# Ten expert chunks issued inside the key search, keys prepared a tile ahead, and shorter runs in the one-hot layout

## The chip, the cores and the metric

The kernel runs on one core of a Trainium2 chip. Its engines are TensorE (PE, matrix products), VectorE (DVE), ScalarE (ACT), GpSimd (POOL) and SyncE (SP, which issues most of the transfers). The metric is the device time of one execution in microseconds, as the median of several runs.

## The reference, cut to what matters

One layer of a transformer-like block: two attention branches and their projections, then a product-key expert layer (PEER). The change lies in the second half. Each of 512 tokens of width 1024 looks up 16 of 16384 experts for each of 8 heads:

```python
def peer_ffn(x, w_q, sub_keys, u, v):          # x: rms-normed tokens
    q = (xb @ w_q).reshape(PEER_BLOCK, PEER_HEADS, 2, PEER_HALF)
    scores = jnp.einsum('thpd,hpkd->thpk', q, sub_keys)
    top_s, top_i = lax.top_k(scores, PEER_TOPK)
    cand_s = top_s[:, :, 0, :, None] + top_s[:, :, 1, None, :]
    cand_i = top_i[:, :, 0, :, None] * PEER_N_KEYS + top_i[:, :, 1, None, :]
    best_s, best_pos = lax.top_k(cand_s, PEER_TOPK)
    expert = jnp.take_along_axis(cand_i, best_pos, axis=-1)
    gate = jax.nn.softmax(best_s, axis=-1)
    act = jax.nn.gelu(jnp.einsum('thkd,td->thk', u[expert], xb), approximate=False)
    return jnp.einsum('thk,thkd->td', (gate * act), v[expert])
```

An expert's number is 128 times its first key plus its second. All is in float32.

## The kernel before

The 512 tokens are four tiles of 128. One tile (`GT`) fetches its experts' rows by indirect transfers, which POOL issues and DVE multiplies. The other three (`DT`, `T` = 384 tokens together) are done densely: all 16384 experts are multiplied for all 384 tokens, 128 experts at a time, and a gate matrix that is zero for experts not chosen selects. A float32 product is three matmuls (`mm3`, L145 to L150) of operands split into a high and a low part: ACT copies the high part, and DVE or POOL subtracts it (`split`, L673 and L674).

**First product, a chunk (`first`).** For one of 128 values `i2` of the one key, a tile `ut` of 512 KB comes over SP's queue (two buffers). ACT makes `uh` in two halves, POOL or DVE makes `ul`, PE forms `pa` in 24 matmuls of 384 columns, and ACT applies the Gelu and writes `ga`. `more(n)` runs the next n chunks ahead of the last loop, with `ul` on POOL. The results `ga` of `AHEAD` = 37 such chunks are kept in SBUF.

**The search** (L582 to L598). For each of 16 chunks `c` of `w_q`: 24 matmuls `mm` of 512 columns, a copy on ACT, four score products `tp<-kt,s` (L592), a copy on ACT, then DVE finds the best sixteen for each tile of tokens (`top16`, L564 to L568), and after every second `c` the best sixteen sums of two keys (`best_sums`).

**Index arithmetic** (L611 to L636). The gate's softmax, with an exponential on ACT (L612), and the positions of the best sums as small integers.

**Retrieval** (`retrieve`, one tile of tokens at a time). ACT spreads positions (`oh`, L646), DVE compares (L647) and multiplies by the keys' numbers (L649), and a tree of four additions (L652, L653) sums 16 places into `ia` and `ib`. After every third step of this generator a chunk is issued: 2 + 8 = 10 chunks in all.

**Token blocks** (L715 to L754). For each dense tile PE transposes keys and gate, ACT makes `sel` of them (L720), and DVE cuts the gate into power of two and two mantissa parts (L725 to L730). Then for each of 8 blocks of 16 tokens DVE makes five tensors of 2048 elements: `o2` (L738), two `ow` (L740), `o1` (L741) and `o1` times `power` (L742). Their layout is (16/`TI`, 128, `TI`), so runs of `TI` = 4 tokens lie side by side. PE multiplies them in 32 matmuls `pg` (L747), which put each gate in its place in the 128 × 128 matrix of experts, ACT copies the matrix out (L750, L751), and SP writes `stage` to DRAM (`spool`). One chunk is issued after every block: 24. Three more follow.

**Last loop** (L799 to L820). For each of the 128 values: `vt` comes in, the gates are multiplied with `ga`, and 18 matmuls `acc` of 512 columns sum the output, with one further chunk beside it while there are some left (91 of 128).

The order of instructions on each engine is set by a scheduler that starts from the order in which the program issues them; each engine works through its own list in order.

Of the kernel before, what the change touches and what calls it, by code (L numbers as in the profile page):

```python
# [8 lines left out]
F32 = mybir.dt.float32  # L9
F32R = mybir.dt.float32r  # L10
# [21 lines left out]
TB = 16  # L32
TI = 4
AHEAD = 37
S2, GAT, WB, UB, VB = 8, 4, 3, 3, 3
# [12 lines left out]
def block_kernel(ctx, tc, x, mix_gain, w_in, gate_bias, q_gain, k_gain, sinks, w_up_a, w_up_b, w_out,  # L48
# [12 lines left out]
    wk = scope(mix, "wk", 2)  # L61
    grp = scope(mix, "grp")
    pmm = scope(mix, "pmm", 4, space=PSUM)
    ptp = scope(mix, "ptp", 2, space=PSUM)
    pz = scope(mix, "pz", 2, space=PSUM)
    gated = ctx.enter_context(ExitStack())
# [503 lines left out]
    def best_sums(h):  # L570
# [8 lines left out]
        for r in range(NT):  # L579
            top16(cs[:, r, :], top[:, r, h, :], pos[:, r, h, :])  # L580

    kt = None  # L582
    norm2(0)
    for c, ps in colsT(w_q, 0, 16, h2T, KD, G, lambda: norm2(1)):
# [15 lines left out]
    dram = ctx.enter_context(tc.tile_pool(name="dram", bufs=1, space=bass.MemoryType.DRAM))  # L600
    xkeep = dram.tile([len(DT), P, D], F32, name="xkeep")
    for i, j in enumerate(DT):
        nc.sync.dma_start(xkeep[i], X[:, NT - 1 - j, :])
    XG = {j: gwk.tile([P, D], F32, name=f"xg{j}") for j in GT}
    for j in GT:
        nc.sync.dma_start(XG[j], X[:, NT - 1 - j, :])
    mix.close()
# [30 lines left out]
    def retrieve(j):  # L638
# [21 lines left out]

    T = P * len(DT)
    SP = P - RES
    upool = scope(ctx, "upool", 2)
    pa_ = scope(ctx, "pa", 2, space=PSUM)
# [3 lines left out]
    def split(pool, src, name, eng, bufs):  # L668

        res = []  # L670
        for b in range(2):
            hi, lo = (pool.tile([P, KD // 2, P], F32R, name=name + n, tag=name + n, bufs=bufs) for n in ("h", "l"))
            A.activation(hi, src[:, 4 * b:4 * b + 4], AF.Copy)  # L673
            eng.tensor_tensor(out=lo, in0=src[:, 4 * b:4 * b + 4], in1=hi.bitcast(F32), op=OP.subtract)  # L674
            res.append((hi, lo))
        return res

    def first(i2, eng=G):

        ut = us.tile([P, KD, P], F32, name="ut", tag="ut", bufs=2)  # L680
        nc.sync.dma_start(ut, peer_ut[i2])
        u = split(us, ut, "u", eng, UB)
        pa = pa_.tile([P, 512], F32, name="pa", tag="pa")
        for k in range(KD):
            mm3(pa[:, :T], u[k // 4], h2T, (SL, k % 4, SL), (SL, k, slice(0, T)), k == 0, k == KD - 1)
        ga = upool.tile([P, T], F32, name="ga", tag="ga", bufs=AHEAD)
        A.activation(ga, pa[:, :T], AF.Gelu)
        return ga

    ahead = {}  # L690

    def more(n):
        for i2 in range(len(ahead), min(len(ahead) + n, AHEAD)):
            ahead[i2] = first(i2)
# [9 lines left out]
    with ExitStack() as st:  # L704
# [9 lines left out]

        for j in DT:  # L715
            pt = pg.tile([P, 4, P], F32, name="pg", tag="pg")
            for i in range(3):
                nc.tensor.transpose(pt[:, i, :], KEYS[j][i].rearrange("p h k -> p (h k)"), ident)
            sel = bw.tile([P, 2, P], F16, name="sel", tag="sel")
            A.activation(sel, pt[:, 0:2, :], AF.Copy)  # L720

            part = bw.tile([P, 2, P], F16, name="part", tag="part")
            two, man = (bw.tile([P, P], F32, name=n, tag=n) for n in ("two", "man"))
            power = bw.tile([P, P], BF16, name="power", tag="power")
            V.tensor_scalar(two.bitcast(I32), pt[:, 2, :].bitcast(I32), 0x7F800000, None, op0=OP.bitwise_and)  # L725
# [3 lines left out]
            V.tensor_copy(part[:, 0, :], man)  # L729
            V.tensor_tensor(out=part[:, 1, :], in0=man, in1=part[:, 0, :], op=OP.subtract)  # L730
            for tb in range(P // TB):
                tg = (NT - 1 - j) * (P // TB) + tb
# [132 lines left out]
```

## Time and profile before

| what | value |
|---|---|
| runs | 1726.94, 1725.89, 1722.54 us; median 1725.89 |
| profiled execution | 1720.6 us; its span 1718.9 us |
| PE busy | 1651.5 us, 96% of the span |
| DVE, ACT, POOL busy | 1282.0 (75%), 745.8 (43%), 582.7 (34%) |
| chain that ended last | PE 81%, DVE 13%, issue 3% |

The chain is followed back from the last instruction, at each step to what released it. "Busy" is the time in which an engine carries out instructions that the profile counts. The clock in a row of windows is the one granted to PE, as a share of 2.4 GHz. In a row of waits the engine and line that waited stand first, behind the arrow the one that ended the wait, then the total in us, the number of waits and the longest.

### The profile page before, as it was taken

Reading aid. Unit: us, or ns where it says so; the run is one execution under the profiler, and the core shown is the slowest. Engines: PE = TensorE matmul, PEld = TensorE weight load, DVE = VectorE, ACT = ScalarE, POOL = GpSimd, SP = SyncE. Lnnn points to the kernel's source line nnn. Section 1 sums busy time; section 2 is a strip of 40 time slices with the busy share of each in tenths; the row PEclk is TensorE's granted clock in tenths of the full one; section 3 lists DMA queues with packets and bytes.
Section 4 is the critical chain, followed back from the end, with each engine's and each line's share of the span. In section 5 each row is a group of like instructions: output and inputs, shape, how many; then the busy total and the mean of one; then the engine's idle time right before and its main releaser. Section 6 shows DMA issues by size and latency. Waiting matters only on the chain.

```text
span 1718.9 us, 24631 instructions
## 1 busy us (share of the span) xinstructions
PE 1651.5 (96%) x8969; PEld 1466.4 (85%) x8969; DVE 1282.0 (75%) x2471; ACT 745.8 (43%) x1457; POOL 582.7 (34%) x446
## 2 busy tenths in 40 slices
PE   6999999999996899989999999999999999999998
PEld 5887777798885798989999999999999999998886
DVE  5444345635999998898897878777777777877874
ACT  4557635533324454545344343343344434443442
POOL 4100011512323654453343434334444343433310
PEclk9999999999998899999999999999999999999999
DMA  4321231123301364657999988888988888877874
GB/s 159 98 75 50 73 89 59 62 87 125 108 1 62 107 205 145 208 171 244 406 372 344 323 277 314 319 290 318 322 281 313 316 295 310 290 269 248 294 234 145
DMA packets 158347, 361.29 MB, mean 210 GB/s; under 512 B 10385, under 2 KB 86161, under 8 KB 156305
## 3 DMA queue, kind: packets, MB, share of 16 engines
q1 hardware_dynamic: 120496, 224.94, 37.5%
q0 software_dynamic: 36864, 134.23, 23.5%
q8 instruction: 70, 1.15, 0.3%
q10 hardware_dynamic: 864, 0.54, 0.1%
q14 instruction: 53, 0.43, 0.1%
HBM read 331.89 MB, written 27.26 MB: 209 GB/s over the span
## 4 chain that ended last, share of the span: by engine, by line
PE 81%; DVE 13%; issue 3%; ACT 1%; POOL 1%; DMA 0%; DVEq 0%; SPq 0%; ACTq 0%; POOLq 0%
PE acc L148 10%; PE acc L150 10%; PE acc L149 10%; PE pa L148 9%; PE pa L150 9%; PE pa L149 9%; PE pg L747 5%; PE mm L149 5%; PE mm L150 5%; PE mm L148 5%; DVE tt L566 1%; PE z L462 1%; DVE oh L652 1%; PE mm L490 1%; DVE idx L568 1%
## 5 line engine op out<-in xcount | busy, mean ns | idle before, releaser
L148 PE MATMUL pa<-h2Th,uh 128*128 128x384 f32 x1024 | 349.3, 341 | 17.6 <-ACT uh L673 17.2
L150 PE MATMUL pa<-h2Th,ul 128*128 128x384 f32 x1024 | 349.6, 341 | 6.8 <-POOL ul L674 6.8
L149 PE MATMUL pa<-h2Tl,uh 128*128 128x384 f32 x1024 | 348.3, 340 | 0.0
L673 ACT ACTIVATE uh<-ut 128x512 fp32r<-128x512 f32 x256 | 160.9, 632 | 323.4 <-PE pa L149 237.1
L148 PE MATMUL acc<-vh,wh 128*128 128x512 f32 x768 | 301.1, 392 | 0.0
L150 PE MATMUL acc<-vh,wl 128*128 128x512 f32 x768 | 299.9, 390 | 0.0
L149 PE MATMUL acc<-vl,wh 128*128 128x512 f32 x768 | 298.6, 389 | 0.0
L762 POOL DMA_INDIRECT row<-peer_u,ex x128 | 175.2, 1369 | 250.0 <-DVE row L774 193.8
L762 POOL DMA_INDIRECT row<-peer_v,ex x128 | 166.5, 1301 | 267.4 <-DVE xg L784 193.0
L673 ACT ACTIVATE vh<-vt 128x512 fp32r<-128x512 f32 x256 | 159.8, 624 | 140.3 <-PE acc L150 136.5
L148 PEld LDWEIGHTS pa<-h2Th,uh 128*128 128x128 f32 x1024 | 195.6, 191 | 23.5 <-ACT uh L673 19.0
L150 PEld LDWEIGHTS pa<-h2Th,ul 128*128 128x128 f32 x1024 | 195.3, 191 | 8.8 <-POOL ul L674 8.8
L149 PEld LDWEIGHTS pa<-h2Tl,uh 128*128 128x128 f32 x1024 | 195.3, 191 | 3.7
L674 POOL TENSOR_TENSOR ul<-ut,uh 128x512 fp32r<-128x512 f32 x74 | 137.0, 1860 | 172.4 <-ACT uh L673 165.4
L674 DVE TENSOR_TENSOR vl<-vt,vh 128x512 fp32r<-128x512 f32 x256 | 176.6, 690 | 23.5 <-ACT vh L673 22.0
L674 DVE TENSOR_TENSOR ul<-ut,uh 128x512 fp32r<-128x512 f32 x182 | 125.5, 690 | 85.4 <-ACT uh L673 85.4
L150 PEld LDWEIGHTS acc<-vh,wl 128*128 128x128 f32 x768 | 144.1, 188 | 32.5
L149 PEld LDWEIGHTS acc<-vl,wh 128*128 128x128 f32 x768 | 144.2, 188 | 27.3
L148 PEld LDWEIGHTS acc<-vh,wh 128*128 128x128 f32 x768 | 144.2, 188 | 26.3
L784 DVE SCALAR_TENSOR_TENSOR xg<-row,wt,xg 128x1024 f32<-128x1024 f32 x128 | 163.7, 1279 | 1.3
L774 DVE SCALAR_TENSOR_TENSOR row<-row,h 128x1024 f32<-128x1024 f32 x128 | 151.4, 1219 | 4.8 <-DMA row<-peer_u,ex 4.7
L158 DVE TENSOR_TENSOR wlo<-w,whi 128x1024 fp32r<-128x1024 f32 x52 | 64.9, 1250 | 85.9 <-ACT whi L157 81.7
(232 smaller groups left out, 2823.5 us busy)
## 6 DMA issues: line engine op xcount, KB each, us to landing
ut<-peer_ut SPq DMA_DIRECT2D x128, 512.0 KB, 4.9
vt<-peer_v SPq DMA_DIRECT2D x128, 512.0 KB, 6.9
spool<-stage SPq DMA_DIRECT2D x24, 960.0 KB, 5.0
gs<-spool SPq DMA_DIRECT2D x15, 1536.0 KB, 9.7
w<-w_in SPq DMA_DIRECT2D x17, 1024.0 KB, 5.4
w<-w_q SPq DMA_DIRECT2D x8, 1024.0 KB, 5.6
w<-w_out SPq DMA_DIRECT2D x4, 1024.0 KB, 5.1
x<-x SPq DMA_DIRECT2D x4, 512.0 KB, 5.8
```

The source lines that it names most:

```text
L148: nc.tensor.matmul(ps, lhsT=l[0][li], rhs=r[0][ri], start=start, stop=False)
L149: nc.tensor.matmul(ps, lhsT=l[0][li], rhs=r[1][ri], start=False, stop=False)
L150: nc.tensor.matmul(ps, lhsT=l[1][li], rhs=r[0][ri], start=False, stop=stop)
L158: eng.tensor_tensor(out=lo, in0=raw, in1=hi.bitcast(F32), op=OP.subtract))
L462: nc.tensor.matmul(z[:, :nk], lhsT=qT[:, h, cols(NT - 1 - j)], rhs=kbT[:, h // 2, row0(j):S], start=True, stop=True)
L490: nc.tensor.matmul(PY[j][s * 64:(s + 1) * 64, h // 2, :], lhsT=vb[:, NT - 1 - j + b, h * DH:(h + 1) * DH], rhs=lt[:, b, :], start=(b == 0) ...
L673: A.activation(hi, src[:, 4 * b:4 * b + 4], AF.Copy)
L674: eng.tensor_tensor(out=lo, in0=src[:, 4 * b:4 * b + 4], in1=hi.bitcast(F32), op=OP.subtract)
L747: nc.tensor.matmul(pp[:, i, :], lhsT=o1[:, q, :, i], rhs=ow[:, s, q, :, i], start=(s == 0), stop=(s == 1))
L762: G.indirect_dma_start(out=t, out_offset=None, in_=src, in_offset=bass.IndirectOffsetOnAxis(ap=ex[:, h, k:k + 1], axis=0))
L774: V.scalar_tensor_tensor(out=t, in0=t, scalar=1.0, in1=h2, op0=OP.mult, op1=OP.mult, accum_out=wt[:, h, k:k + 1]))
L784: V.scalar_tensor_tensor(out=xj, in0=t, scalar=wt[:, h, k:k + 1], in1=xj, op0=OP.mult, op1=OP.add))
```

## The change

`EARLY` = 10 chunks are issued in the search, one after each of `c` = 4 to 13. Their `ga` lie in a pool of their own, `early`, where the rows of the residual (`X`, pool `grp`) lay. For that, the rows are copied out (`xkeep`, `xg`) ahead of the second norm, and their pool has a stack of its own that ends there. The PSUM pool of `pa` opens before the search, in the place of a pool of the attention that now closes earlier. The tree of four additions becomes one `tensor_reduce`. In the retrieval a chunk is issued after every second step, 2 + 12 = 14 in all. In the token blocks it is one after every second block, 12 in all, with `ul` on DVE; two more follow, so `AHEAD` is 38. The preparation of keys is now a function, `parts`, which is called for the next tile in the fourth block of the one before, with two buffers for what it makes. The layout's `TI` falls from 4 to 2; the matmuls of `pg` still come four tokens at a time.

```diff
-TI = 4
-AHEAD = 37
+TI = 2
+AHEAD = 38
+EARLY = 10
...
     gated.close()
+    early = scope(ctx, "early", side="right")
     us = scope(ctx, "us", 2, side="right")
+    pa_ = scope(ctx, "pa", 2, space=PSUM, side="right")
...
+        if i2 % AHEAD < EARLY:
+            ga = early.tile([P, T], F32, name="ga", tag="ga", bufs=EARLY)
+        else:
+            ga = upool.tile([P, T], F32, name="ga", tag="ga", bufs=AHEAD - EARLY)
...
         if c % 2:
             best_sums(c // 2)
+        if 4 <= c < 4 + EARLY:
+            more(1)
     mix.close()
...
-            for n in (8, 4, 2):
-                V.tensor_tensor(out=oh[:, :, :, 0:n], in0=oh[:, :, :, 0:n], in1=oh[:, :, :, n:2 * n], op=OP.add)
-            V.tensor_tensor(out=dst, in0=oh[:, :, :, 0], in1=oh[:, :, :, 1], op=OP.add)
+            V.tensor_reduce(out=dst, in_=oh, axis=AX.X, op=OP.add)
...
     more(2)
     for j in DT + GT:
         for i, _ in enumerate(retrieve(j)):
-            if i % 3 == 0:
+            if i % 2 == 0:
                 more(1)
...
-        for j in DT:
+        def parts(j):
+
...
+            return sel, part, power
+
+        now = parts(DT[0])
+        for n, j in enumerate(DT):
+            sel, part, power = now
             for tb in range(P // TB):
...
-                more(1)
+                if tb % 2 == 0:
+                    more(1, V)
+                if tb == 3 and n + 1 < len(DT):
+                    now = parts(DT[n + 1])
```

Three places in the order. On PE in the search, around the score product (`tp<-kt,s`) of a late `c`; before:

```order
L150 MATMUL mm<-h2Th,wlo 128x512
L148 MATMUL mm<-h2Th,whi 128x512
L592 MATMUL tp<-kt,s_4807 128x128 x4
L149 MATMUL mm<-h2Tl,whi 128x512
L150 MATMUL mm<-h2Th,wlo 128x512
```
After, the same place for `c` = 13:

```order
L152 MATMUL mm<-h2Tl,whi 128x512
L153 MATMUL mm<-h2Th,wlo 128x512
L151 MATMUL pa<-h2Th,uh 128x384
L152 MATMUL pa<-h2Tl,uh 128x384
L153 MATMUL pa<-h2Th,ul 128x384
L151 MATMUL pa<-h2Th,uh 128x384
L643 MATMUL tp<-kt,s_5156 128x128 x4
```
The score products stood among `mm` matmuls alone; now they stand among `pa` matmuls of a chunk, 244 of which come before the last score product.

On DVE in the retrieval, the first tile; before (`i16` holds the places 0 to 15, `idf` the keys' numbers):

```order
L647 TENSOR_TENSOR oh_5146<-oh_5146,i16_3676 128x2048
L649 TENSOR_TENSOR oh_5146<-oh_5146,idf_5043 128x2048
L652 TENSOR_TENSOR oh_5146<-oh_5146 128x128x8
L652 TENSOR_TENSOR oh_5146<-oh_5146 128x128x4
L647 TENSOR_TENSOR oh_5191<-oh_5191,i16_3676 128x2048
L652 TENSOR_TENSOR oh_5146<-oh_5146 128x128x2
L649 TENSOR_TENSOR oh_5191<-oh_5191,idf_5043 128x2048
L653 TENSOR_TENSOR ia1_5144<-oh_5146 128x128
```
After:

```order
L692 TENSOR_TENSOR oh_5519<-oh_5519,i16_3692 128x2048
L694 TENSOR_TENSOR oh_5519<-oh_5519,idf_5419 128x2048
L692 TENSOR_TENSOR oh_5598<-oh_5598,i16_3692 128x2048
L696 TENSOR_REDUCE ia1_5517<-oh_5519 128x128
L694 TENSOR_TENSOR oh_5598<-oh_5598,idf_5419 128x2048
L696 TENSOR_REDUCE ib1_5518<-oh_5598 128x128
```
The four additions of a tree are replaced by one row, and less stands between the products of one half and of the next.

On DVE in the token blocks; before, two blocks:

```order
L740 TENSOR_TENSOR ow_5723<-o2_5722,part_5529 128x2048 x2
L741 TENSOR_TENSOR o1_5721<-rep_5521,sel_5527 128x2048
L738 TENSOR_TENSOR o2_5813<-rep_5521,sel_5527 128x2048
L742 TENSOR_TENSOR o1_5721<-o1_5721,power_5532 128x2048
L740 TENSOR_TENSOR ow_5814<-o2_5813,part_5529 128x2048 x2
L741 TENSOR_TENSOR o1_5812<-rep_5521,sel_5527 128x2048
```
After, from the third block's products on:

```order
L759 TENSOR_TENSOR ow_6183<-o2_6182,part_6026 128x2048 x2
L760 TENSOR_TENSOR o1_6181<-rep_6018,sel_6024 128x2048
L608 TENSOR_TENSOR ul_6240<-ut_6233,uh_6239 128x512
L761 TENSOR_TENSOR o1_6181<-o1_6181,power_6029 128x2048
L757 TENSOR_TENSOR o2_6273<-rep_6018,sel_6024 128x2048
L760 TENSOR_TENSOR o1_6272<-rep_6018,sel_6024 128x2048
L759 TENSOR_TENSOR ow_6274<-o2_6273,part_6026 128x2048 x2
L761 TENSOR_TENSOR o1_6272<-o1_6272,power_6029 128x2048
```
And on ACT after, ahead of these blocks, with the first copy of `gres` that belongs to them:

```order
L734 ACTIVATE sel_6024<-pg_6020 128x256
L607 ACTIVATE uh_6239<-ut_6233 128x512
L607 ACTIVATE uh_6395<-ut_6393 128x512
L624 ACTIVATE ga_6123<-pa_6098 128x384
L607 ACTIVATE uh_6399<-ut_6393 128x512
L770 ACTIVATE gres_5441<-pg_6044 128x8x4
L771 ACTIVATE stage_6035<-pg_6044 128x120x4
```
The row of `ul` stands among the products of DVE, where none stood; the `uh` that it reads (6239) stands on ACT ahead of the copies of the first block.

## Rows read from the trace of the kernel before

**Rows 1.** Busy us (x instructions) of PE, PEld, DVE, ACT, POOL; clock; DMA, by stage.

```profile
417.00:525.00 108.00, 107.11 (x548) 90.28 (x547) 105.64 (x733) 35.65 (x51) 34.66 (x17) 1.00 0.20 64
525.00:593.00 68.00, 44.05 (x199) 40.06 (x198) 65.21 (x124) 30.33 (x38) 33.89 (x19) 0.80 0.21 69
593.00:798.00 205.00, 191.75 (x1337) 186.04 (x1336) 185.99 (x137) 101.34 (x264) 99.18 (x52) 0.95 0.62 183
```

**Rows 2.** Waits in 510 to 798: us in total, times, longest.

```profile
PE pa L148 <- ACT uh L673: 17.2, 5, 10.2
...
ACT gate L612 <- DVE gate L611: 13.0, 1, 13.0
PE pg L747 <- DVE o L742: 12.8, 3, 5.3
DVE two L725 <- ACT sel L720: 12.6, 2, 6.8
```

**Rows 3.** A 5-us window after the search, columns as in rows 1.

```profile
530.00:535.00 5.00, 0.00 (x0) 0.00 (x0) 4.93 (x36) 0.58 (x2) 0.00 (x0) 0.50 0.00 0
```

**Rows 4.** PE timeline at three edges: start, us, what.

```profile
509.70 1.16 PE L592 MATMUL tp<-kt,s 128*128 128x128 f32 x8 [0.75 <-ACT s L589]
...
793.77 3.93 PE L747 MATMUL pg<-ow,o 128*128 128x128 f16 x32
...
810.89 0.40 PE L148 MATMUL acc<-vh,wh 128*128 128x512 f32 x1
```

**Rows 5.** DVE timeline at the edges of the stages.

```profile
523.93 0.47 DVE L564 MAX8 vals<-s 128x8 f32<-128x128 f32 x2
...
533.72 0.67 DVE L611 TENSOR_TENSOR gate<-top 128x512 f32<-128x512 f32 x1
...
540.42 1.21 DVE L647 TENSOR_TENSOR oh<-oh,i 128x2048 bf16<-128x2048 bf16 x1
...
593.49 0.28 DVE L725 TENSOR_SCALAR two<-pg 128x128 int32<-128x128 int32 x1
```

**Rows 6.** DVE and POOL timelines in the first token blocks.

```profile
607.82 1.21 DVE L741 TENSOR_TENSOR o<-rep,sel 128x2048 bf16<-128x2048 f16 x1
608.95 1.21 DVE L738 TENSOR_TENSOR o<-rep,sel 128x2048 f16<-128x2048 f16 x1
...
602.24 2.28 DVE L742 TENSOR_TENSOR o<-o,power 128x2048 bf16<-128x2048 bf16 x1
...
602.03 1.41 POOL L674 TENSOR_TENSOR ul<-ut,uh 128x512 fp32r<-128x512 f32 x1
```

**Rows 7.** Groups of DVE in 593 to 798: busy us, mean ns, idle before.

```profile
L740 DVE TENSOR_TENSOR ow<-o,part 128x2048 f16<-128x2048 f16 x48 | 85.9, 1827 | 1.0 <-PE pg L747 1.0
```

**Rows 8.** Last loop, tile wh, with and without chunks: min/median/max ns, first and last start.

```profile
L814 ACT ACTIVATE wh<-ga x3: 525/525/527, 1005.6 to 1022.2; 128x384 fp32r<-128x384 f32 x3
...
L814 ACT ACTIVATE wh<-ga x3: 525/525/527, 1560.8 to 1569.0; 128x384 fp32r<-128x384 f32 x3
```

**Rows 9.** Groups of DVE in 533 to 593.5.

```profile
L652 DVE TENSOR_TENSOR oh<-oh 128x1024 bf16<-128x1024 bf16 x8 | 9.8, 1219 | 0.0
...
L652 DVE TENSOR_TENSOR oh<-oh 128x512 bf16<-128x512 bf16 x8 | 6.8, 854 | 0.1
L652 DVE TENSOR_TENSOR oh<-oh 128x256 bf16<-128x256 bf16 x8 | 6.8, 845 | 0.0
L653 DVE TENSOR_TENSOR ia<-oh 128x128 f32<-128x128 bf16 x4 | 2.8, 693 | 0.0
L653 DVE TENSOR_TENSOR ib<-oh 128x128 f32<-128x128 bf16 x4 | 1.8, 438 | 0.1
...
L614 DVE TENSOR_REDUCE gsum<-gate 128x32 f32<-128x512 f32 x1 | 0.7, 677 | 0.0
```

**Rows 10.** Section 5 of the page: the splits of ut on POOL and DVE.

```profile
L674 POOL TENSOR_TENSOR ul<-ut,uh 128x512 fp32r<-128x512 f32 x74 | 137.0, 1860 | 172.4 <-ACT uh L673 165.4
...
L674 DVE TENSOR_TENSOR ul<-ut,uh 128x512 fp32r<-128x512 f32 x182 | 125.5, 690 | 85.4 <-ACT uh L673 85.4
```

More of the change, by code (lines that the diff above doesn't have):

```diff
@@ L61, in block_kernel @@
     wk = scope(mix, "wk", 2)
-    grp = scope(mix, "grp")
+    xrows = ctx.enter_context(ExitStack())
+    grp = scope(xrows, "grp")
     pmm = scope(mix, "pmm", 4, space=PSUM)
     ptp = scope(mix, "ptp", 2, space=PSUM)
-    pz = scope(mix, "pz", 2, space=PSUM)
+    zs = ctx.enter_context(ExitStack())
+    pz = scope(zs, "pz", 2, space=PSUM)
     gated = ctx.enter_context(ExitStack())
@@ L501, in block_kernel @@
     attn.close()
+    zs.close()
     gwk = scope(ctx, "gwk", side="right")
@@ L542, in block_kernel @@
     run(rows(w_out, 0, D, mg, o_done))
+    dram = ctx.enter_context(tc.tile_pool(name="dram", bufs=1, space=bass.MemoryType.DRAM))
+    xkeep = dram.tile([len(DT), P, D], F32, name="xkeep")
+    for i, j in enumerate(DT):
+        nc.sync.dma_start(xkeep[i], X[:, NT - 1 - j, :])
+    XG = {j: gwk.tile([P, D], F32, name=f"xg{j}") for j in GT}
+    for j in GT:
+        nc.sync.dma_start(XG[j], X[:, NT - 1 - j, :])
+    xrows.close()
     def norm2(p):
@@ L580, in best_sums, with split, first, more @@
             top16(cs[:, r, :], top[:, r, h, :], pos[:, r, h, :])
+    T = P * len(DT)
+    upool = None
+    def split(pool, src, name, eng, bufs):
+        res = []
+        for b in range(2):
+            hi, lo = (pool.tile([P, KD // 2, P], F32R, name=name + n, tag=name + n, bufs=bufs) for n in ("h", "l"))
+            A.activation(hi, src[:, 4 * b:4 * b + 4], AF.Copy)
+            eng.tensor_tensor(out=lo, in0=src[:, 4 * b:4 * b + 4], in1=hi.bitcast(F32), op=OP.subtract)
+            res.append((hi, lo))
+        return res
+    def first(i2, eng=G):
+        ut = us.tile([P, KD, P], F32, name="ut", tag="ut", bufs=2)
+        nc.sync.dma_start(ut, peer_ut[i2])
+        u = split(us, ut, "u", eng, UB)
+        pa = pa_.tile([P, 512], F32, name="pa", tag="pa")
+        for k in range(KD):
+            mm3(pa[:, :T], u[k // 4], h2T, (SL, k % 4, SL), (SL, k, slice(0, T)), k == 0, k == KD - 1)
+        if i2 % AHEAD < EARLY:
+            ga = early.tile([P, T], F32, name="ga", tag="ga", bufs=EARLY)
+        else:
+            ga = upool.tile([P, T], F32, name="ga", tag="ga", bufs=AHEAD - EARLY)
+        A.activation(ga, pa[:, :T], AF.Gelu)
+        return ga
+    ahead = {}
+    def more(n, eng=G):
+        for i2 in range(len(ahead), min(len(ahead) + n, AHEAD)):
+            ahead[i2] = first(i2, eng)
     kt = None
@@ L598, in block_kernel @@
             best_sums(c // 2)
[L600 to L606, printed above, removed]
+        if 4 <= c < 4 + EARLY:
+            more(1)
     mix.close()
@@ L658, in retrieve @@
             V.scalar_tensor_tensor(out=ROWS[j], in0=ib, scalar=128.0, in1=ia, op0=OP.mult, op1=OP.add)
-    T = P * len(DT)
     SP = P - RES
     upool = scope(ctx, "upool", 2)
-    pa_ = scope(ctx, "pa", 2, space=PSUM)
     gres = upool.tile([P, RES, T], F32, name="gres", bufs=1)
     spool = dram.tile([SP // OCT, P, T // TB, OCT, TB], F32, name="spool")
[L668 to L694, printed above, removed]
     more(2)
@@ L718, in block_kernel @@
                 nc.tensor.transpose(pt[:, i, :], KEYS[j][i].rearrange("p h k -> p (h k)"), ident)
-            sel = bw.tile([P, 2, P], F16, name="sel", tag="sel")
+            sel = bw.tile([P, 2, P], F16, name="sel", tag="sel", bufs=2)
             A.activation(sel, pt[:, 0:2, :], AF.Copy)
-            part = bw.tile([P, 2, P], F16, name="part", tag="part")
+            part = bw.tile([P, 2, P], F16, name="part", tag="part", bufs=2)
             two, man = (bw.tile([P, P], F32, name=n, tag=n) for n in ("two", "man"))
-            power = bw.tile([P, P], BF16, name="power", tag="power")
+            power = bw.tile([P, P], BF16, name="power", tag="power", bufs=2)
             V.tensor_scalar(two.bitcast(I32), pt[:, 2, :].bitcast(I32), 0x7F800000, None, op0=OP.bitwise_and)
@@ L742, in block_kernel @@
                 V.tensor_tensor(out=o1, in0=o1, in1=spread(power[:, ts]), op=OP.mult)
-                for q in range(TB // TI):
-                    pp = pg.tile([P, TI, P], F32, name="pg", tag="pg")
-                    for i in range(TI):
+                for q in range(TB // 4):
+                    pp = pg.tile([P, 4, P], F32, name="pg", tag="pg")
+                    for i in range(4):
+                        t, k = divmod(4 * q + i, TI)
                         for s in range(2):
-                            nc.tensor.matmul(pp[:, i, :], lhsT=o1[:, q, :, i], rhs=ow[:, s, q, :, i],
+                            nc.tensor.matmul(pp[:, i, :], lhsT=o1[:, t, :, k], rhs=ow[:, s, t, :, k],
                                              start=(s == 0), stop=(s == 1))
```

## Prediction

> **What bounds the kernel now.** I read the stage windows first, then the waits between 510 and 798 us, then the timelines of TensorE (PE) and VectorE (DVE) at the stages' edges. The kernel is a PE kernel with one hole. In [rows 1] three stretches stand under one another. While the best keys are sought (417 to 525) PE is busy for 107.11 of 108 us, and so is DVE, with 105.64. In 525 to 593 (index arithmetic and retrieval) PE is busy for only 44.05 of 68 us, at a mean clock of 0.80. In 593 to 798 (token blocks) it is 191.75 of 205 at 0.95. So of these 381 us PE lies idle for 38, and further time goes at the lower clock. The waits say whose fault that is: PE waits 17.2 us for ACT's `uh` in 5 pieces, the longest 10.2, and 12.8 us for DVE's `o` in 3 pieces [rows 2]. The long one is a chain: ACT has the gate's exponential in its queue and waits 13.0 us for DVE's gate [rows 2], the `uh` stand behind it, and PE does nothing in 530 to 535, where the clock is 0.50, which is 1.2 GHz [rows 3].
>
> DVE is why. The last score product on PE ends at 510.9 (509.70 + 1.16) [rows 4], but DVE only begins the last chunk's top sixteen at 523.93 and the gate at 533.72 [rows 5]: it is behind by 22.9 us, 9.8 of it for that last chunk and its best sums. After that DVE does index arithmetic to 540.42 and the retrieval to 593.49 [rows 5], and the token blocks run until PE's last `pg` row, at 793.77 for 3.93 us, ends at 797.7. The first `acc` follows at 810.89 [rows 4], 13.2 us later, and from there on PE is full.
>
> DVE in the token blocks is slowed by POOL. A 2048-element operation takes 1.21 us (starts 1.13 apart, 607.82 and 608.95) where POOL is idle, and 2.28 at 602.24, where POOL splits `ul` from 602.03 on [rows 6]. The mean of the `ow` products is 1.827 us [rows 7].
>
> **The change part by part.** All is reckoned against the profiled run's own 1720.6 us (span 1718.9); the median of the runs, 1725.89, is 5.3 above it.
>
> *A chunk's price on PE.* In the last loop the `wh` of one expert block follows the last by 8.3 us while a chunk is among them (1005.6 to 1022.2, two steps) and by 4.1 after the last chunk (1560.8 to 1569.0) [rows 8]. A chunk of 24 `pa` matmuls is thus 4.2 us, 0.174 each.
>
> *Ten chunks into the search.* The order shows 244 `pa` matmuls ahead of the last score product, none before. They add 244 × 0.174 = 42.5 us to a stage in which PE was full, so that product ends at 553.4 instead of 510.9. DVE's work there stays the same, some 106 us, but now has 150 to be done in, so its lag falls to the last chunk's own: 0.7 for ACT's copy and 9.8, that is 10.5 instead of 22.9, a gain of 12.4. The POOL splits (two an iteration, of 1.4 us each [rows 6]) and ACT's two `uh` lie beside PE's 10.7 us an iteration. The ten `ut` transfers stand behind `w_q`'s on SP; they are asked for long ahead, so I cost them at nothing. If that cover fails, it is rival D. The moved `xkeep` and `xg` transfers read finished rows and cost nothing.
>
> *Index arithmetic* stays at 6.7 us (533.72 to 540.42).
>
> *Retrieval, 53.1 us before.* Eight trees of four adds took 9.8 + 6.8 + 6.8 + 2.8 + 1.8 = 28.0 us, 3.5 each [rows 9], beside POOL. One `tensor_reduce` over 2048 elements does not occur before. The nearest row reduces 512 in 0.677 us [rows 9], so four times that, 2.7, is the upper end; the 1.21 of a 2048-element product is the lower end, 1.2. I take 2.5, near the upper one since it is the same operation: −1.0 × 8 = −8. Were the adds free of POOL (3.5 × 1.21 / 2.28 = 1.9), the reduce would cost 0.6 × 8 = 5 us more than they do; POOL keeps its splits in this stage, so I don't take that. Now three chunks go with each tile. PE needs 14 × 4.2 = 59 us for the stage's 14 chunks, POOL 28 splits at 1.86 [rows 10] = 52, and from 553.4 to the loop's start DVE needs 10.5 + 6.7 + 45 = 62. They are so close that ACT's queue will couple them: I give back 3 (my estimate) and take 48 for the retrieval, a gain of 5.
>
> The Trainium skill ("VectorE: DVE Perf Modes", Rules for kernel authors) calls `tensor_reduce` the slowest operation of DVE, to be expected at one element a cycle, and advises restructuring, which speaks against this edit. By that rule the reduce would be some 2.2 us, an estimate, and the sum would fall by 2 more, since the adds it replaces are held up by POOL here.
>
> *Token blocks, 593.5 to 797.7 = 204.2 us before.* The splits of the twelve chunks left here move from POOL to DVE. 24 blocks × 5 operations × 1.135 = 136.3. Of the 24 `ul` 21 stand inside the loop at 0.69 [rows 10] = 14.5. Three preparations of keys, each five operations on 128 elements, are some 2 us each by my estimate: 6 to 7, taken as 7. The last 32 `pg` add 3.9. Sum 161.7, a gain of 42.5. With the keys prepared a tile ahead the 12.6 us that DVE waited in two pieces for `sel` [rows 2] go, which is in this sum, since it has no waits. PE needs 24 × 3.93 + 12 × 4.2 = 145 there, so DVE sets the pace. ACT, with 101.34 us of work in this stage before [rows 1] and half the chunks now, lies below that too. The inner runs of these operations fall from four elements to two (`TI`): no row shows runs of two. Between 1.13, the price of runs of four, and 2.28, which a disturbed one takes, I take 1.135, because the order keeps count and size. The other end is rival A.
>
> *Last loop.* 38 instead of 37 chunks are done ahead: one less beside `acc`, −4.2. The 13.2 us between the last `pg` and the first `acc` stay.
>
> *Sum.* 553.4 + 10.5 + 6.7 + 48 = 618.6; + 161.7 = 780.3; + 13.2 = 793.5 against 810.9: −17.4. With −4.2 it is −21.6 us: 1699.0 for a run like the profiled one, **1704** for the median. The gains of 59.9 (12.4 + 5 + 42.5) less the 42.5 of the chunks moved ahead give the same 17.4.
>
> **The rivals.**
> - **A, slower: runs of two cost DVE its rate.** All 120 operations of the token blocks would go at about 2.28 instead of 1.21: +128 us, 1832. It decides from 21.6 / 120 = 0.18 us an operation. Against it: rows with runs of four are at the full rate. The Trainium skill ("Vector Engine (DVE) Microarchitecture Reference", on performance modes) asks for a unit step and more than one element in the inner dimension for 16-bit data, which a run of two fulfils; no run here shows it. Chance 0.05.
> - **B, slower: DVE waits in its own queue.** Each `ul` in the token blocks waits for ACT's `uh`, which needs a buffer that PE must free, and all products of the next block stand behind it, so that PE then waits for `o`. If this chain is met in full it is 32 `pg` (3.93), 10 matmuls (1.7) and `uh` (0.6, like `ul` on DVE or less), 6.3 us a pair of blocks: 12 × 6.3 = 76, 1780. It decides from 21.6 / 12 = 1.8 us a pair. For it: before, `uh` waits for PE often and POOL absorbs that; against it: in the new order `uh` stands a pair of blocks ahead of its `ul`. Chance 0.07.
> - **C, no change: the retrieval stays as slow as before.** ACT's queue again holds `uh` behind the gate, PE waits 10 us, the clock falls as in [rows 3], and the trees' gain (5) is not had: at a clock of 0.80 for 62 us 12 more are lost. All of it is 27, half of it 14, which gives 1718 to 1731, about 1726. Against it: 332 matmuls now stand between the last score product and the keys, and the lag is half. Chance 0.10.
> - **D, the ten chunks don't fit into the search.** `ut` or the split comes late and a chunk takes what it took in 510 to 593, ten in 83 us, 8.3 each: +41, 1745. Chance 0.03.
>
> **How the numbers follow.** My forecast has the remaining 0.75, with a range of its own of 1690 to 1720: below by a reduce at 1.2 (−10) and no coupling (−3), above by half of C. Faster or slower means by over 0.3% (below 1720.7 or above 1731.1), about what a measurement of this kernel can tell from no change. Faster 0.75; the same is C, 0.10; slower A, B and D, 0.15. For 8 in 10 the range takes in C: 1688 to 1730.
>
> **What would show it.** The last `tp<-kt,s` at about 553 with PE full before it; the gate on DVE some 11 us later, and no 10-us wait of PE for `uh`; `tensor_reduce` near 2.5; the five operations of a block at 1.21 each with no POOL beside them; the first `acc` near 793. A mean of the block operations over 1.4, `ul` rows of DVE with waits for `uh` of over 2 us a pair, or a search that ends after 560 would make it wrong.

## The result, and the profile after

The changed kernel takes 1704.33 us (median; 1702.74 to 1708.35), the kernel before beside it 1725.01: the ratio is 0.9884, with a 95% interval of 0.9863 to 0.9906, that is some 20 us or 1.2% faster. Its profiled execution took 1704.63 us (span 1702.9), 16.0 less than the one of before. The forecast was 1704 for the median, and 1699.0, that is −21.6, for the profiled execution. The sum came out nearly right; of its terms two did not, in opposite directions, and the part that the change is named for, the chunks in the search, turned out to be a loss.

The windows of the changed kernel, by stage (busy us and instructions of PE, PEld, DVE, ACT and POOL, then PE's clock, the DMA share and GB/s); they answer to [rows 1]:

```profile
417.00:554.50 137.50, 137.50 (x729) 121.01 (x728) 105.21 (x725) 47.72 (x76) 56.77 (x33) 1.00 0.24 81
554.50:573.00 18.50, 16.31 (x92) 15.38 (x90) 17.41 (x83) 10.24 (x14) 7.43 (x5) 1.00 0.26 85
573.00:617.50 44.50, 38.27 (x191) 36.68 (x192) 40.64 (x25) 25.86 (x33) 29.81 (x18) 0.88 0.27 95
617.50:631.00 13.50, 13.50 (x80) 13.36 (x80) 3.51 (x5) 4.80 (x10) 8.36 (x7) 1.00 0.63 216
631.00:788.00 157.00, 112.24 (x1047) 103.95 (x1047) 151.59 (x156) 76.00 (x228) 13.95 (x3) 0.88 0.64 189
```
The search is now 137.5 us, all of them with PE busy. The hole behind it (44.05 of 68 us in [rows 1]) is nearly filled: PE is busy for 16.31 of 18.5 and 38.27 of 44.5, then for 13.50 of 13.50. The idle time has moved on into the token blocks, where PE is busy for 112.24 of 157 and DVE for 151.59.

PE's timeline at the edges, to be held against [rows 4] (start, duration, what):

```profile
553.19 1.16 PE L643 MATMUL tp<-kt,s 128*128 128x128 f32 x8
...
785.84 2.01 PE L767 MATMUL pg<-ow,o 128*128 128x128 f16 x32
...
798.98 0.50 PE L151 MATMUL acc<-vh,wh 128*128 128x512 f32 x1
```
And DVE's, to be held against [rows 5]:

```profile
566.28 0.67 DVE L656 TENSOR_TENSOR gate<-top 128x512 f32<-128x512 f32 x1
...
572.68 1.23 DVE L692 TENSOR_TENSOR oh<-oh,i 128x2048 bf16<-128x2048 bf16 x1 [0.51 <-ACT oh L691]
...
616.98 0.57 DVE L701 SCALAR_TENSOR_TENSOR ex<-ib,ia 128x128 int32<-128x128 f32 x1
622.74 1.93 DVE L608 TENSOR_TENSOR ul<-ut,uh 128x512 fp32r<-128x512 f32 x1 [5.20 <-ACT uh L607]
...
630.15 0.69 DVE L608 TENSOR_TENSOR ul<-ut,uh 128x512 fp32r<-128x512 f32 x1 [4.63 <-ACT uh L607]
630.81 0.29 DVE L739 TENSOR_SCALAR two<-pg 128x128 int32<-128x128 int32 x1
```
The last score product ends at 554.35 (553.19 + 1.16), the gate follows 11.9 us later, the first comparison of the retrieval begins at 572.68, and the last row of the retrieval (`ex`) ends at 617.55. Then DVE stands still for most of 13 us: its next rows are `ul`, which wait 5.20 and 4.63 us for `uh`, and the key preparation (`two`) begins only at 630.81. From there the blocks run to the end of the last `pg`, 787.85, and the first `acc` is at 798.98 instead of 810.89.

What happens in these 13 us is seen on the other engines: a window of all engines from the last score product to the transposes of the keys (columns as above), the last of the three transposes on PE, and ACT's next rows.

```profile
554.40:626.20 71.80, 63.38 (x333) 60.83 (x332) 60.72 (x109) 39.49 (x52) 44.11 (x29) 0.93 0.29 97
```
```profile
626.38 0.27 PE L732 MATMUL pg<-ident,gate 128*128 128x128 f32 x1
```
```profile
629.49 0.63 ACT L607 ACTIVATE uh<-ut 128x512 fp32r<-128x512 f32 x1 [4.69 <-DMA ut<-peer_ut]
630.03 0.47 ACT L624 ACTIVATE ga<-pa 128x384 f32<-128x384 f32 x1
630.40 0.38 ACT L734 ACTIVATE sel<-pg 128x256 f16<-128x256 f32 x1
```
PE works through the chunks issued ahead of the transposes and ends the transposes at 626.65, 9.1 us after DVE's last row of the retrieval. ACT makes `sel` of them only at 630.40, since an `uh` that waits for a `ut` transfer stands ahead of it. So some 9 of the 13 us are PE's chunks and some 4 are ACT's queue with that transfer.

The waits between 510 and 800 (total, times, longest), against [rows 2]:

```profile
PE pg L767 <- DVE o L761: 32.1, 12, 4.5
...
DVE ul L608 <- ACT uh L607: 10.0, 3, 5.2
...
PE pa L151 <- ACT uh L607: 5.4, 3, 2.9
...
ACT gate L657 <- DVE gate L656: 2.8, 1, 2.8
```
ACT's wait for the gate fell from 13.0 to 2.8 us, and with it PE's longest wait for `uh`, from 10.2 to 2.9. In the token blocks PE now waits 32.1 us for DVE, where it waited 12.8.

DVE's groups in the blocks and the reduce in the retrieval (busy us, mean ns), against [rows 7] and [rows 9]:

```profile
L759 DVE TENSOR_TENSOR ow<-o,part 128x2048 f16<-128x2048 f16 x48 | 56.7, 1220 | 0.0
L761 DVE TENSOR_TENSOR o<-o,power 128x2048 bf16<-128x2048 bf16 x24 | 29.3, 1220 | 0.0
...
L608 DVE TENSOR_TENSOR ul<-ut,uh 128x512 fp32r<-128x512 f32 x24 | 16.9, 738 | 10.0 <-ACT uh L607 10.0
...
L696 DVE TENSOR_REDUCE ia<-oh 128x128 f32<-128x2048 bf16 x4 | 9.1, 2277 | 0.0
```
All 2048-element operations of the blocks take 1.22 us, where the `ow` products took 1.827 in the mean. The price is 24 `ul` of 0.738 us. The reduce takes 2.28 us; all eight lie between 2.27 and 2.29, also the one that begins at 576.22 while POOL has splits from 575.42 to 580.88.

### The profile page after: what moved, and what is told of

Read it like the earlier page. It is cut to its first block, busy times and chain, and to the rows that moved or that the text cites. A ratio compares the mean times of both kernels' runs of the same rounds, so it can differ in the third digit from the quotient of the medians.

```text
span 1702.9 us, 24586 instructions
## 1 busy us (share of the span) xinstructions
PE 1622.9 (95%) x8969; PEld 1436.1 (84%) x8969; DVE 1240.0 (73%) x2469; ACT 740.0 (43%) x1457; POOL 535.8 (31%) x424
## 4 chain that ended last, share of the span: by engine, by line
PE 84%; DVE 6%; issue 3%; DMA 3%; POOL 2%; ACT 1%; DVEq 0%; SPq 0%; ACTq 0%; POOLq 0%
PE acc L151 10%; PE acc L153 10%; PE acc L152 10%; PE pa L153 9%; PE pa L151 9%; PE pa L152 9%; PE mm L153 6%; PE mm L152 6%; PE mm L151 6%; DVE ow L759 2%; POOL ul L608 2%; PE z L465 1%; DMA ut<-peer_ut 1%; PE mm L493 1%; PE tp L643 1%
## 5 line engine op out<-in xcount | busy, mean ns | idle before, releaser
L785 POOL DMA_INDIRECT row<-peer_v,ex x128 | 170.7, 1333 | 247.4 <-DVE xg L807 179.6
L607 ACT ACTIVATE vh<-vt 128x512 fp32r<-128x512 f32 x256 | 159.8, 624 | 137.5 <-PE acc L153 136.9
L608 DVE TENSOR_TENSOR ul<-ut,uh 128x512 fp32r<-128x512 f32 x204 | 140.8, 695 | 85.9 <-ACT uh L607 84.9
L153 PEld LDWEIGHTS acc<-vh,wl 128*128 128x128 f32 x768 | 144.1, 188 | 32.3
L608 POOL TENSOR_TENSOR ul<-ut,uh 128x512 fp32r<-128x512 f32 x52 | 85.1, 1643 | 207.5 <-ACT uh L607 203.0
```

What stands on the lines that cost most here:

```text
L153: nc.tensor.matmul(ps, lhsT=l[1][li], rhs=r[0][ri], start=False, stop=stop)
L785: G.indirect_dma_start(out=t, out_offset=None, in_=src, in_offset=bass.IndirectOffsetOnAxis(ap=ex[:, h, k:k + 1], axis=0))
```

## The experiments

The theory behind the forecast: DVE's line of work (search, lag, arithmetic, retrieval, blocks) sets when the last loop begins, and chunks are something that PE does beside it. The rivals: PE's amount of work sets it, or the chunks in the search are what brings the gain. Ratios below are to the kernel before in the same series; the changed kernel's is 0.9884, and "us against the changed kernel" is the quotient of the two ratios times 1704.

### Without the chunks in the search

```diff
-        if 4 <= c < 4 + EARLY:
-            more(1)
...
-                if tb % 2 == 0:
-                    more(1, V)
+                more(1, V)
```

> The changed kernel without its main part: no chunk in the key search; the ten chunks are issued in the token blocks instead, one after every block, all with ul on DVE; nothing else differs. Theory (DVE's line of work sets the time from the search to the first acc, and PE has 45 idle us in the token blocks): the search ends 42 us earlier, DVE's lag grows back by 12, the token blocks grow by 12 chunks x 2 x 0.69 = 17 us, the retrieval becomes free of its wait or keeps it: the first acc comes 13 to 24 us earlier, at 775 to 786, and the time is 1680 to 1692, faster than both kernels. Rival (chunks in the search are what brought the gain, since they fill PE there): the time goes back to 1720 or more. Third: PE's work only moves, the time stays within 1700 to 1708.

Measured: 1681.19 us, ratio 0.9767 (0.9742 to 0.9792), 20 us *faster* than the changed kernel. This is the theory's number and the end of both rivals. The hole of PE behind the search is back (PE waits 13.3 us in one piece for `uh`), and the kernel is faster all the same. The score products end at 513.3, the gate is at 533.01, the first `acc` at 777.9. The entry to the blocks shows the same wait as in the changed kernel (DVE's timeline):

```profile
583.25 0.29 DVE L699 SCALAR_TENSOR_TENSOR ex<-ib,ia 128x128 int32<-128x128 f32 x1
587.45 0.69 DVE L608 TENSOR_TENSOR ul<-ut,uh 128x512 fp32r<-128x512 f32 x1 [3.90 <-ACT uh L607]
589.53 0.72 DVE L608 TENSOR_TENSOR ul<-ut,uh 128x512 fp32r<-128x512 f32 x1 [1.39 <-ACT uh L607]
594.90 0.69 DVE L608 TENSOR_TENSOR ul<-ut,uh 128x512 fp32r<-128x512 f32 x1 [4.65 <-ACT uh L607]
595.55 0.29 DVE L737 TENSOR_SCALAR two<-pg 128x128 int32<-128x128 int32 x1
```
The retrieval is done at 583.5, the blocks begin at 595.55, and three `ul` in between wait 3.90, 1.39 and 4.65 us. The blocks then last until 766.9, 171.4 us instead of 157.0, for twelve chunks more: 1.2 us a chunk, about DVE's two `ul` (2 × 0.69), and not the 4.2 of PE.

### Chunks in the search alone

The kernel before, with ten chunks in the search and the pools for it, fifteen in the blocks (`tb` 0, 2, 4, 6, 7) and nothing else of the change.

```diff
+        if 4 <= c < 4 + EARLY:
+            more(1)
...
-                more(1)
+                if tb in (0, 2, 4, 6, 7):
+                    more(1)
```

> The kernel before with one part of the change alone: ten chunks in the search (with the pools that this needs), 10 in the retrieval as before, 15 instead of 24 in the token blocks with ul on POOL, two behind them; runs of four, the tree, the keys at a tile's start and 37 chunks as before. Theory (in the search PE and DVE are both full, so a chunk there costs its 4.2 us, and in the blocks DVE sets the pace, so that a chunk less there saves only what POOL takes from DVE): the search ends 42 later, the lag gives back 11, nine chunks less on POOL beside DVE give back 9 x 2 x 1.1 = 20: 5 to 15 us slower than before, 1.003 to 1.009. Rival (the chunks in the search are a gain by themselves): 10 us or more faster, under 0.994. No difference would mean that the blocks give back all 42.

Measured: 1739.35 us, ratio 1.0101 (1.0084 to 1.0118), 17 us slower than before. The sign is the theory's, the size a little over its range. PE's timeline:

```profile
553.46 1.16 PE L643 MATMUL tp<-kt,s 128*128 128x128 f32 x8
...
814.11 3.95 PE L768 MATMUL pg<-ow,o 128*128 128x128 f16 x32
...
834.65 1.65 PE L151 MATMUL acc<-vh,wh 128*128 128x512 f32 x3 [6.66 <-ACT vh L607]
```
The search ends 43.8 us later than in [rows 4]. Up to the last `pg` 20.4 of these are left: 9 are given back until the blocks begin (628.12 against 593.49; the lag gives back 11, the retrieval takes 2 of it), and 14 by the blocks (189.9 us instead of 204.2); the way to the first `acc` then takes 16.6 us instead of 13.2. So both ways of asking agree: ten chunks in the search cost 17 to 20 us.

### Fewer chunks in the retrieval, more in the blocks

On top of the kernel without chunks in the search:

```diff
-            if i % 2 == 0:
+            if i % 3 == 0:
                 more(1)
...
-                more(1, V)
+                more(2 if tb % 6 == 5 else 1, V)
```

> The kernel without chunks in the search (e3_no_early) with six fewer chunks... exactly: a chunk after every third step of the retrieval instead of every second (8 instead of 12), one chunk more in one block of each tile (27 instead of 24), and one behind the blocks. In e3_no_early DVE ended the retrieval at 583.5 and the blocks began at 595.6, since PE was still at the chunks ahead of the transposes. Theory (DVE's line counts): the 12 us of waiting go, three chunks more cost DVE 4 us: 4 to 10 us faster than e3_no_early, a ratio of 0.971 to 0.975 to the kernel before, 1671 to 1678. Rival (PE, with 162 us of work in blocks of 175, becomes the bound): as e3_no_early, 1679 to 1684.

(In words: four chunks fewer in the retrieval, 8 instead of 12; 27 instead of 24 in the blocks.) Measured: 1676.59 us, ratio 0.9714 (0.9697 to 0.973), by the ratios 9 us faster than without this step (the intervals allow 2 to 16) and some 29 us faster than the changed kernel. DVE's timeline at the entry:

```profile
587.08 0.28 DVE L699 SCALAR_TENSOR_TENSOR ex<-ib,ia 128x128 int32<-128x128 f32 x1
...
588.37 0.29 DVE L737 TENSOR_SCALAR two<-pg 128x128 int32<-128x128 int32 x1 [0.41 <-ACT sel L732]
```
The 12 us between the last row of the retrieval and `two` are 1.0 now. The transposes of the keys end on PE at 573.84 here, 13.5 us ahead of the end of the retrieval; without this step they ended at 592.07, 8.5 us behind it. So that wait was in the main PE's backlog of chunks, behind which the transposes stand. The blocks take 174.1 us (588.37 to 762.49), and the first `acc` comes at 774.86, only 3.1 us earlier than without this step: in these two executions the gate is 3.0 us later here, the retrieval, the blocks and the way to the first `acc` are longer by 0.8, 2.8 and 1.3, and of the 11 us won at the entry 3 are left.

### Runs of four again, and in the kernel before runs of two

```diff
-TI = 2
+TI = 4
```

> The changed kernel with one part undone: the one-hot layout has runs of four tokens again (TI = 4). In the trace of the changed kernel the 32 pg matmuls of a block take 2.01 us, 3.93 before; DVE's operations take 1.22 in both. Theory (DVE sets the pace of the token blocks): pg returns to 3.9, PE's work there rises by 24 x 1.92 = 46 us, but PE idled for 45 of these 157 us, so the loop stays within 0 to 4 us of its 157 and the time within 1703 to 1709. Rival (the cheaper pg is what the change really brought): the time rises by 20 us or more, to 1725 or above, that is back to the kernel before.

Measured: 1715.11 us, ratio 0.9957 (0.9938 to 0.9975), 12.6 us slower than the changed kernel: more than the theory's 0 to 4, less than the rival's 20. Two rows of `pg` and the clock in their windows, with runs of four:

```profile
636.95 3.94 PE L767 MATMUL pg<-ow,o 128*128 128x128 f16 x32 [4.60 <-DVE o L761]
...
648.67 3.94 PE L767 MATMUL pg<-ow,o 128*128 128x128 f16 x32
```
```profile
637.00:641.00 4.00, 3.89 (x32) 3.60 (x32) 4.00 (x4) 2.05 (x7) 0.00 (x0) 0.50 0.00 0
...
649.00:652.50 3.50, 3.50 (x32) 3.45 (x31) 3.50 (x4) 1.98 (x6) 0.00 (x0) 1.00 1.07 333
```
and with runs of two, in the changed kernel:

```profile
638.63 3.59 PE L767 MATMUL pg<-ow,o 128*128 128x128 f16 x32 [3.94 <-DVE o L761]
...
650.53 2.01 PE L767 MATMUL pg<-ow,o 128*128 128x128 f16 x32
```
```profile
640.00:642.00 2.00, 2.00 (x21) 1.96 (x19) 2.00 (x3) 1.61 (x5) 0.00 (x0) 0.50 0.00 0
...
650.00:652.50 2.50, 2.50 (x36) 2.34 (x36) 2.50 (x3) 1.30 (x6) 0.00 (x0) 0.95 1.03 303
```
With runs of four 32 `pg` take 3.94 us, at a clock of 0.50 as at 1.00. With runs of two they take 3.59 at 0.50 and 2.01 where it is 0.95 in the mean of the window; the last row of the blocks takes 2.01 at 1.00. So with runs of four something other than the clock sets the time, and with runs of two the clock does. All `pg` together keep PE busy for 94.9 us with runs of four and 57.7 with runs of two, 37 less, of which 12 reach the end of the blocks: these last 168.7 us instead of 157.0, and DVE waits 8.6 us in two pieces for `sel`, whose transposes stand behind the longer `pg`.

In the kernel before the same edit, `TI` = 2, alone:

> The kernel before with one part of the change: runs of two tokens (TI = 2), four tokens still in one PSUM tile. Theory (DVE, slowed by POOL, sets the pace of the token blocks before): pg falls to 2.0 us, DVE's operations keep 1.2 to 2.3, and the time falls by no more than the waits of PE behind it, 0 to 8 us: 1717 to 1725. Rival (pg's length is what matters): 46 us of PE fall out of a stage in which PE was busy for 192 of 205, and the time falls by 20 us or more, to 1705 or less. If runs of two cost DVE its rate after all when POOL works beside it, the mean of the ow products rises over 2.0 us.

Measured: 1719.78 us, ratio 0.9987 (0.9977 to 0.9997), 2 us faster. `pg` is 2.01 at full clock there too, PE's wait for DVE's `o` in the blocks rises to 31.9 us, and the time hardly moves: PE is busy for 159.87 us of the blocks instead of 191.75, and they last 204 us as before, with DVE busy for 182.84. DVE, held up by POOL, set the pace. The shorter `pg` is worth something only once DVE is free.

### Runs of one and of eight

> The changed kernel with runs of one token (TI = 1): the third rung beside runs of two and four. Theory of DVE's rate (runs of one lose it): the 2048-element operations of the blocks go from 1.22 to about 2.2 us, 120 of them give +115 to +130 us, 1815 to 1835. Rival: 1.22 stays, and the time with it, 1700 to 1708. For PE: if pg follows the distance between the elements that it reads (4 tokens apart 3.94 us, 2 apart 2.01), one apart gives 1.0 to 2.0; if 2.01 is the floor of 32 such matmuls, 2.0.

> The changed kernel with runs of eight tokens (TI = 8), the fourth rung: elements that PE reads for pg lie eight apart. In the runs so far 32 pg matmuls took 3.94 us at four apart, whether the clock was 1.2 or 2.4 GHz, and 2.01 at 2.4 GHz and 3.59 at 1.2 GHz at two apart. Theory (reading is limited by the distance, by bytes): about 7.9 us, PE becomes the bound of the blocks with 24 x 7.9 + 50 = 240 us, 80 us more, 1780 to 1800. Rival (from four apart on each element costs one access, whatever the distance): 3.94 and the time of the kernel with runs of four, 1710 to 1720. DVE's operations stay at 1.22.

One execution each: 1832.94 us with runs of one, 1820.27 with runs of eight. With runs of one DVE loses half its rate:

```profile
L759 DVE TENSOR_TENSOR ow<-o,part 128x2048 f16<-128x2048 f16 x46 | 103.3, 2284 | 0.0
```
and with runs of eight PE is the bound (timeline of PE and the clock in that row's window, then the group of DVE that waits for it):

```profile
666.34 7.70 PE L767 MATMUL pg<-ow,o 128*128 128x128 f16 x32
```
```profile
666.40:674.00 7.60, 7.60 (x34) 4.87 (x34) 0.00 (x0) 1.98 (x6) 0.00 (x0) 0.50 0.29 82
```
```profile
L760 DVE TENSOR_TENSOR o<-rep,sel 128x2048 bf16<-128x2048 f16 x22 | 26.9, 1223 | 68.2 <-PE pg L767 68.2
```
Of runs of one most rows follow idle times of PE and took 3.59 to 3.60 us, as with runs of two at a clock of 0.50. The last row ran at full clock (timeline and window):

```profile
916.22 1.96 PE L767 MATMUL pg<-ow,o 128*128 128x128 f16 x32
```
```profile
916.20:918.20 2.00, 2.00 (x34) 1.99 (x34) 0.23 (x1) 1.33 (x6) 0.00 (x0) 1.00 0.38 154
```
Eight apart 32 `pg` take 7.7 us, at a clock of 0.50 as at 0.87 in the mean (691.85 to 699.54, 7.69 us); four apart they take 3.94; at full clock two apart take 2.01 and one apart 1.96. The time goes with the distance between the elements that PE reads, down to two apart, and no further. Of the four sizes runs of two are the one at which neither engine pays. The time with eight lies 20 us over the range expected; the mean clock in its blocks (632 to 860) was 0.64, and a `pa` row there takes 0.46 us in the mean instead of 0.34, which I had not reckoned with.

### The tree in place of the reduce

```diff
-            V.tensor_reduce(out=dst, in_=oh, axis=AX.X, op=OP.add)
+            for n in (8, 4, 2):
+                V.tensor_tensor(out=oh[:, :, :, 0:n], in0=oh[:, :, :, 0:n], in1=oh[:, :, :, n:2 * n], op=OP.add)
+            V.tensor_tensor(out=dst, in0=oh[:, :, :, 0], in1=oh[:, :, :, 1], op=OP.add)
```

> The changed kernel with the tree of four additions in place of tensor_reduce. The reduce takes 2.28 us, the tree took 3.5 beside POOL's splits. Theory: DVE's work in the retrieval rises by 8 x 1.2 = 10 us, but DVE waits about 10 us there, at the entry of the token blocks, for PE's chunks: 0 to 4 us, 1703 to 1709. Rival (DVE's work there counts in full): 8 to 12 us more, 1712 to 1717. If the trees run free of POOL they take 1.9 and the time is the same or 3 us less.

Measured: 1716.94 us, ratio 0.9973 (0.996 to 0.9985), 15 us slower than the changed kernel. Neither 0 to 4 nor, quite, the rival's 8 to 12. Waits from 566 to 641:

```profile
DVE ul L608 <- ACT uh L607: 13.4, 3, 9.7
ACT oh L691 <- DVE ia L698: 13.0, 3, 5.7
```
The retrieval itself, from its first comparison to the end of `ex`, takes 53.0 us instead of 44.9. My reason for 0 to 4 was that DVE waits for PE's chunks afterwards anyway. It does (13.4 us for `uh` in three pieces, and 10.0 in the changed kernel), but the chunks come later as well: ACT waits 13.0 us for DVE's `ia` before it can spread the next tile, and the `uh` of the chunks stand behind that in its queue. So the backlog moves along with DVE, and of the 12.6 us by which the first `acc` is later (811.60 against 798.98) 8.1 are the retrieval itself. That ACT's queue is why the chunks come later is argued from these rows and not tested apart: at the end of the retrieval two `uh` also wait for `ut` transfers, 7.99 and 3.55 us.

### The splits of the blocks on POOL

```diff
-                    more(1, V)
+                    more(1)
```

> The changed kernel with one part undone: in the token blocks ul is made by POOL again instead of DVE. In the changed kernel every operation of the blocks takes 1.22 us and DVE's own 24 ul are 17 us. Theory (POOL's splits hold up DVE's operations beside them): each ul on POOL, 1.3 to 2.3 us long, takes about 1.1 us from a DVE operation beside it, so 24 of them cost 26 us and save 17; the mean of the ow products rises to 1.4 to 1.9 and the time by 5 to 15 us, to 1707 to 1717. Rival (what counts is that DVE's queue is kept free of ul and of its waits for uh): the time falls, to 1690 to 1700.

Measured: 1721.15 us, ratio 0.998 (0.9965 to 0.9995), 17 us slower, a little over the range. DVE's `ow` products and POOL's splits in the blocks:

```profile
L759 DVE TENSOR_TENSOR ow<-o,part 128x2048 f16<-128x2048 f16 x48 | 61.9, 1328 | 6.4 <-PE pg L767 6.4
```
```profile
L608 POOL TENSOR_TENSOR ul<-ut,uh 128x512 fp32r<-128x512 f32 x26 | 56.5, 2185 | 56.8 <-ACT uh L607 51.1 <-PE pa L153 3.7 <-ACT stage L771 1.9
```
The operations of the blocks add up to 161.0 us (61.9 + 33.5 + 33.3 + 32.3) instead of 144.6, so the splits on POOL take 16.4 us from DVE, and the `ul` off DVE give back 16.9 (3.3 of it ahead of the blocks). As work for DVE the two ways are about equal. The blocks take 173.1 us instead of 157.0 all the same, and 18 us instead of 11.1 pass from the last `pg` to the first `acc`. What is left is the chain: a split on POOL takes 2.185 us instead of 0.738, PE waits for it and for `o` (6.4 and 40.8 us), and DVE waits 6.4 us for PE. That these waits make up the whole difference is argued from the rows, not shown; the term from which the time was foretold is at most half of it.

This run also shows what DVE's wait ahead of the blocks is not. Here no `ul` stands in DVE's queue between `ex` and `two`, and DVE waits as long:

```profile
631.64 0.29 DVE L739 TENSOR_SCALAR two<-pg 128x128 int32<-128x128 int32 x1 [14.18 <-ACT sel L734]
```
So it is not the place of `ul` in DVE's queue that holds up the entry, but `sel`, which comes late.

### The keys at a tile's start

`parts` called at the start of each tile instead of in the fourth block of the one before:

```diff
-            sel, part, power = now
+            sel, part, power = parts(j)
...
-                if tb == 3 and n + 1 < len(DT):
-                    now = parts(DT[n + 1])
```

> The changed kernel with one part undone: the keys of a tile are prepared at that tile's start, not in the fourth block of the tile ahead. Before, DVE waited 12.6 us in two pieces for sel there. Theory: two of the three preparations wait again for the transposes behind PE's work and for ACT's copies, 4 to 6 us each: 1710 to 1717. Rival (PE has room in the blocks, so the transposes come at once): 0 to 4 us, 1702 to 1708.

Measured: 1708.38 us, ratio 0.9902 (0.9886 to 0.9919). The interval overlaps that of the changed kernel, so 3 us are what it may be worth, if anything; it is the rival's range, not mine. In the profiled execution the blocks take 162.8 us instead of 157.0.

## Why the prediction was right, point by point

| term | forecast, us | measured, us |
|---|---|---|
| last score product ends | 553.4 | 554.35 |
| lag until the gate | 10.5 | 11.9 |
| index arithmetic | 6.7 | 6.4 |
| retrieval, to the start of `two` | 48 | 58.1 |
| token blocks, to the end of the last `pg` | 161.7 | 157.0 |
| to the first `acc` | 13.2 | 11.1 |
| first `acc` | 793.5 | 799.0 |
| last loop against before | −4.2 | −4.1 |

- **The chunks in the search.** PE full, no waits, 42.5 us forecast and 43.5 measured (554.35 − 510.86). The lag fell to 11.9 us, where 10.5 was forecast. Rival D is out: PE was busy for 137.50 of 137.50 us.
- **The retrieval** is the term that was mis-sized, by 10 us. Its own work took 44.9 us, 3 less than the 48. What I gave back for "coupling", 3 us, was 13: I had set 59 us of chunks beside 62 of DVE and not followed who waits at the end. DVE's line was right (63.2 us from the last score product to the end of `ex`). PE's was not: the transposes that DVE needs next stand behind 332 `pa` matmuls, which are 57.8 us at 0.174 and took 71.8, since PE was idle for 8.4 us of them and ran at a mean clock of 0.93. PE's line was thus the longer of the two, and behind it came 4 us of ACT's queue. It looks like a part of rival B, since the waits are written against `ul` (10.0 us for `uh`), but with the splits on POOL DVE waits 14.2 us there without a `ul` in its queue. With 8 chunks in the retrieval instead of 12 the transposes come in time and the wait goes; that run has no chunks in the search either.
- **The reduce** took 2.28, not 2.5. The Trainium skill's rule of one element a cycle ("VectorE: DVE Perf Modes", Rules for kernel authors), 2.2 by my estimate, agrees with the trace. Its advice there to consider restructuring does not pay here: the tree is four operations, 3.2 us together in the run with the tree (25.9 for eight) beside POOL's splits, which did not lengthen the reduce, and the kernel with it is 15 us slower.
- **The token blocks.** 1.22 us an operation, no POOL, 24 `ul`: as reckoned. Some 3 us less were needed for the preparations and the rows at the end, and 1.9 for the last `pg`. What I had not seen at all is that runs of two halve `pg`. I had costed the layout for DVE only. By the run with runs of four it is worth 12.6 us: without it the change would have come to about 1717 us, still within the range stated, but for my reasons alone 13 us off. With `pg` as long as I had costed it the blocks took 168.7 us, 7 more than forecast, and DVE, which was to set the pace, waited there for `sel`.
- **Rival A** names a real mechanism at the wrong place. With runs of one the operations take 2.284 us and the kernel 1833 us, where I had 2.28 and 1832 for runs of two. Runs of two keep the full rate, as the Trainium skill ("Vector Engine (DVE) Microarchitecture Reference", Performance modes) has it for more than one element; the trace agrees with 1.220.
- **Rival C** didn't come: ACT's wait for the gate is 2.8 us.
- **The whole.** In the profiled executions the gain is 16.0 us, not 21.6; the medians differ by 20.7, because the profiled execution of before was 4.4 us quicker than its median and the one of after 0.3 us slower. So that the median came out at 1704 is luck by some 5 us, and it is luck too that an effect I had not seen (the short `pg`) made up for a wait I had not seen (the entry to the blocks). What the forecast did not say, though its sum held it: gains of 59.9 against 42.5 us for chunks moved into a full stage. A chunk there costs 4.2 us, and in the blocks two `ul` (2 × 0.69); both numbers stood in the prediction, and they tell that the chunks are better left in the blocks. That is what the kernel without them shows, 20 us faster, and the one with the backlog removed as well, 29 us.

Undone one by one, the parts are worth: ten chunks in the search, −20 us (a loss); POOL's splits in the blocks moved to DVE, 17; the reduce, 15; runs of two, 13; keys ahead, about 3, which is not clear of the noise. By the intervals each is uncertain by some 4 to 6 us, so that they add up to 28 against 20 measured proves nothing by itself. But they are not independent: the `pg` that became short is worth 2 us in the kernel before and 13 in the changed one.

## What to carry to other kernels

When work can be done beside several stages, price it in each by the engine that sets that stage's pace: a full stage charges the whole of it, a stage in which another engine leads charges only what falls on that engine. At the end of a stage that has been filled, look at what the next one needs first, and what stands ahead of that in its engine's queue. A change of a layout is to be costed for every engine that reads it.

## What was not expected of the hardware

32 matmuls of 128 × 128 in 16-bit types took 7.7 us where the elements that PE reads lie eight apart (16 bytes), 3.94 where four, 2.01 where two, and 1.96 where they lie side by side; the last three at full clock. Four apart the time was the same at either level of the clock (3.94 at 1.2 and at 2.4 GHz); eight apart no row ran at full clock throughout, and the time was the same at 0.50 and at a mean of 0.87; two apart it followed the clock (3.59 and 2.01). Whether it is the operand that is loaded or the one that streams was not told apart: both have the same distance in these runs.
